# An encoder trunk on one core: turning a unit's products after the next block-sum step, and a third block-sum step in the sixteen-tile down pairs

## The chip, the cores and the metric

The kernel runs on one core of one Trainium2 chip. The metric is the device time of one execution in microseconds (us), the median of several runs. The core has five engines with queues of their own: TensorE (PE; PEld is its weight load), VectorE (DVE), ScalarE (ACT), GpSimd (POOL) and SyncE (SP). SP and POOL issue the transfers from the device's memory here.

## The reference

Two residual layers on a sequence of 256 tokens of width 2048, all in float32. Layer 0 mixes tokens by grouped-query attention, layer 1 by a gated linear recurrence. After each mixer comes the same gated feed-forward block, and only this block is touched by the change:

```python
D_MODEL, SEQ, DEPTH = 2048, 256, 2
D_FF = -(-8 * D_MODEL // (3 * 256)) * 256          # 5632

def swiglu(h, w_gate, w_up, w_down):
    return (jax.nn.silu(h @ w_gate) * (h @ w_up)) @ w_down

for i in range(DEPTH):
    h = rms_norm(x, norm_mix[i])
    x = x + (attention_mixer(h, ...) if i % 2 == 0 else recurrent_mixer(h, ...))
    x = x + swiglu(rms_norm(x, norm_ffn[i]), w_gate[i], w_up[i], w_down[i])
```

## The kernel before

**Three products for one.** A float32 number is split into a high part (rounded to the type that TensorE takes) and a low part (the rest). A product of two such numbers is three matmuls: high by high, high by low, low by high (`product` in `project_pair`). Each weight that comes from memory is therefore cast on ScalarE (`hi`) and subtracted on VectorE (`lo`), in `load_half`. A *half* is one load of 512 KB: two tiles of 128 rows by 512 columns. There are five buffers each for `raw`, `hi` and `lo`, so the preparation can run some halves ahead of TensorE.

**A pair.** `project_pair` computes two neighbouring outputs of 512 columns (j = 0 and 1) for all 256 tokens, in four accumulators. A *step* n takes the operand tiles 2n and 2n+1. A plain step has two halves, one for each j, with four products (12 matmuls) in each. `pair_plan` puts the first steps of a pair through both outputs together, and the rest first for j = 0, then for j = 1, so that output 0 can be finished early (`done(0, ...)`) while output 1 still runs.

**A block-sum step** replaces the eight products of a step by seven, from sums and differences of blocks, as Strassen's and Winograd's schemes do. Such a step needs sums of the weight blocks, which `seven_forms` prepares: one half comes through SP, the sum of two blocks through POOL, which loads one half and adds another to it during the transfer (tile `sr`, two buffers, fetched two block-sum steps ahead by `fetch_next`), and one quarter through SP again (`wx`). Three more blocks are made on VectorE (L307, L311, L312), and all are split into high and low parts (`wxh` and `wxl` are the three combined blocks, cast by L310 and L314, subtracted by L315 and L316; one buffer each). It also needs sums of the token blocks, made once for each step by `x_forms` (L325 to L330). Four of the seven products go to banks of their own, and after the last block-sum step of the pair `merge` (L382 to L386) combines them into `fg` and `fu`.

**The feed-forward block** (`ffn`) has 44 tiles of hidden features, in three groups (`PARTS`): 12, 16 and 16. A *unit* is a pair whose outputs are a gate and an up projection of four tiles, and so a group has 3, 4 or 4 units. All units but a layer's first have block-sum steps at n = 1, 3, 5, the first unit at 3 and 5. At its end, L842 adds the banks to the gate and a Silu follows on ScalarE, and L845 and L846 make the products `u` (tile `fu`). The products stand with tokens in the partitions, and the down projection wants features there. So they are *turned*: a transpose of 32 x 32 blocks on VectorE (L515), 16 copies of 32 x 256 between partitions on ScalarE (L523), then the split into a high and a low part (L857, L858). Then `x_forms` makes the token sums where the down pairs want them.

After a group's units come its two *down pairs* (`down`, c = 0 and 2), whose results are added to the residual stream `x_tok`. They have 6 steps in the first group (no block sums) and 8 in the others, with block-sum steps at n = 2 and 5. The second pair of layer 0's last group (`alone`) has none, since the next norm starts behind it.

**The order of the work.** TensorE's instructions run in the order in which the program writes them. Those of the other engines are ordered by a scheduler at build time, which takes from what is ready, the earlier written first, by its own timeline; each engine then runs its list in order. Two lines of order are given by hand: within the block, the weight casts on ScalarE follow each other, and the subtractions on VectorE too (`in_line`, `line`). `follow(i, j)` puts i behind j on the same engine.

Of the kernel before, what the change touches and what calls it, by code (L numbers as in the profile page):

```python
# [12 lines left out]
F32 = mybir.dt.float32  # L13
F32R = mybir.dt.float32r
AF = mybir.ActivationFunctionType
ALU = mybir.AluOpType
AX = mybir.AxisListType

P = 128
# [54 lines left out]
def trunk(ctx, tc, w, out):  # L74
# [79 lines left out]
    def down_plan(n, alone):  # L154
        if alone:
            return pair_plan(range(n), 0)
        return pair_plan(range(n), SHORT - 2 if n == SHORT else 1 + TWO[-1])
# [1 line left out]
    seven_at, ffn_ends = [], []  # L159

    def down_seven(n, alone):
        return () if alone or n == SHORT else TWO

    def ffn_order(l, base):
        units = [wide(f"w_gate{l}"), wide(f"w_up{l}")]
# [34 lines left out]
    def half():  # L200
        n = taken[0]
        taken[0] += 1
        if n == 0:
            load_x(0, 2)
            scale_x(0)
            return load_half(*order[n], 4, partial(load_x, 2, 2))
        if n == 1:
            scale_x(1)
            return load_half(*order[n], 2)
        if n < KT // 2:  # L210
            if n % 2 == 0:
                load_x(2 * n, 4)
            if n < KT // 2 - 1:
                scale_x(n)
        if n == KT // 2 - 2:
            scale_x(n + 1)
            load_tables()
        if n == KT // 2 + 2:
            tiles = load_half(*order[n])
            token_squares(1)  # L220
            return tiles
        return load_half(*order[n])
# [57 lines left out]
    def flat(t):  # L280
        return t.rearrange("p (k c) f -> p k (c f)", k=2)
# [39 lines left out]
    def x_forms(h0, h1, tag):  # L321
# [8 lines left out]
        dve.tensor_tensor(t[:, 1], y[:, 4:, :], t[:, 0].bitcast(F32), ALU.subtract)  # L330
        return [(t[:, 0, i, :], t[:, 1, i, :]) for i in range(4)]

    def project_pair(xs, forms, plan, middle, done):
        banks = [[], []]
        begun = set()

        def bank(j, a):
            while len(banks[j]) <= a:
                banks[j].append(new_acc())
            return banks[j][a]  # L340

        def product(acc, x, wt, last=False):
            for i, (a, b) in enumerate(((x[0], wt[0]), (x[0], wt[1]), (x[1], wt[0]))):
                pe.matmul(acc, a, b, start=id(acc) not in begun, stop=last and i == 2)  # L344
                begun.add(id(acc))
            step()
            step()

        def tokens(k, a):
            return [xs[k][:, o + a * P : o + (a + 1) * P] for o in (0, S)]  # L350

        seven = [n for n, cols in plan if n in forms]
        for n, cols in plan:
            if n in forms:
                s1, s2, s3, s4 = forms[n]
                b11, b21, t3, b22, t1, t2, t4 = seven_forms()
                if n == seven[0]:
                    p1, q6, q5, q7 = (ps_m.tile([P, WIDE], F32, tag="pm", name=nm("pm")) for _ in range(4))
                last = n == seven[-1]
                product(p1, tokens(2 * n, 0), b11, last)  # L360
                product(bank(0, 0), tokens(2 * n + 1, 0), b21)
                product(bank(1, 0), s4, b22)
                product(q7, s3, t3, last)
                product(q5, s1, t1, last)
                product(q6, s2, t2, last)
                product(bank(0, 1), tokens(2 * n + 1, 1), t4)
                if last:
                    middle(p1, q5, q6, q7)
                continue
            end = n == plan[-1][0]  # L370
            for j in cols:
                half()
                hi, lo = (flat(t) for t in newest["tiles"])
                for a in range(2):
                    for k in range(2):
                        product(bank(j, a), tokens(2 * n + k, a), (hi[:, k, :], lo[:, k, :]), end and k == 1)
                if end:
                    done(j, banks[j])
# [129 lines left out]

    def turned(src, both=True, behind=None, whole=False):
        b = fp[0].tile([P, 2, FOUR, P], F32, tag="tb", name=nm("tb"))
        f = fp[0].tile([P, 8, FOUR, 32], F32, tag="tf", name=nm("tf"))
        if whole:
            dve.transpose(b, src)  # L515
        for a in () if whole else range(2):
            dve.transpose(b[:, a, :, :], src[:, a, :])
        for q in range(4):
            for i in range(4):
                o, y = f[32 * i : 32 * i + 32, q::4, :, :], b[32 * q : 32 * q + 32, :, i, :]  # L520
                y = y.rearrange("p a (k t) -> p a k t", k=FOUR)
                turn = dve.tensor_copy if i % 2 and both else act.copy
                n = turn(o, y)  # L523
                if behind is not None:
                    follow(n, behind[i % 2])
        return f[:].rearrange("p q k t -> p k q t") if whole else [f[:, :, k, :] for k in range(FOUR)]

    fp = []

# [27 lines left out]
                norm.add(c)  # L557


    def down(xs, forms, norm=None, end=False):  # L560
        for c in (0, 2):
            def middle(*banks):
                g, u = merge(*banks)
                for j, t in enumerate((g, u)):
                    for a in range(2):
                        y = x_tok[:, a, c + j, :]
                        dve.tensor_tensor(y, y, t[:, a, :], ALU.add)

            def done(j, accs):
                for a in range(2):  # L570
                    n = 2 if end and c + j == NCOL - 1 else 1
                    for i in range(n):
                        sl = slice(i * WIDE // n, (i + 1) * WIDE // n)
                        y = x_tok[:, a, c + j, sl]
                        dve.tensor_tensor(y, y, accs[a][:, sl], ALU.add)
                        if end:
                            sync.dma_start(out=out[:, a, c + j, sl], in_=y)
                if norm is not None:
                    norm.add(c + j)

            alone = norm is not None and c > 0
            project_pair(xs, {} if alone else forms, down_plan(len(xs) // 2, alone), middle, done)


    prev = [None]
# [202 lines left out]
    def act_tiles():  # L788
        return xp.tile([P, FOUR, 2 * S], F32R, tag="act", name=nm("act"), bufs=4)
# [40 lines left out]
    def ffn(norm, nxt):  # L830
        coming[:] = [k for k in seven_at if taken[0] <= k < ffn_ends[taken[0] > ffn_ends[0]]]
        for _ in range(2):
            fetch_next()

        def unit(hid, forms, parts, i):
            got = []

            def done(j, accs):
                g, u = got
                for a, acc in enumerate(accs):  # L840
                    if j == 0:
                        dve.tensor_tensor(g[:, a, :], acc, g[:, a, :], ALU.add)  # L842
                        table_act(g[:, a, :], g[:, a, :], AF.Silu, scale=norm.rt[:, a : a + 1])
                    else:
                        dve.tensor_tensor(u[:, a, :], acc, u[:, a, :], ALU.add)  # L845
                        dve.scalar_tensor_tensor(u[:, a, :], u[:, a, :], norm.rt[:, a : a + 1], g[:, a, :], ALU.mult, ALU.mult)  # L846

            project_pair(norm.xs, {n: norm.forms[n] for n in unit_seven(i)}, unit_plan(i), lambda *banks: got.extend(merge(*banks)), done)
            if i == 0:
                n = THREE[0]  # L850
                norm.forms[n] = x_forms(norm.xs[2 * n], norm.xs[2 * n + 1], f"nf{n}")
            u = got[1]
            first = len(hid)
            f = turned(u, False, whole=True)
            h = act_tiles()
            hi, lo = (h[:, :, o : o + S].rearrange("p k (q t) -> p k q t", t=32) for o in (0, S))
            act.copy(hi, f)  # L857
            dve.tensor_tensor(lo, f, hi.bitcast(F32), ALU.subtract)  # L858
            hid.extend(h[:, k, :] for k in range(FOUR))
            for k, n in enumerate(TWO):  # L860
                if parts == KT and first <= 2 * n < len(hid):
                    forms[n] = x_forms(hid[2 * n], hid[2 * n + 1], f"hf{k}")

        line.update(act=None, dve=None)
        for p, n in enumerate(PARTS):
            hid, forms = [], {}
            for i in range(n // FOUR):
                unit(hid, forms, n, sum(PARTS[:p]) // FOUR + i)
            last = p == len(PARTS) - 1
            if last and nxt is not None:  # L870
                ln_exp_tables()
            down(hid, forms, nxt if last else None, last and nxt is None)
        line.clear()

    nr = Norm("norm_mix", KT)
# [218 lines left out]
```

## Time and profile before

| what | value |
|---|---|
| median of 3 runs | 1989.0 us (1987.55 to 1989.62) |
| the profiled execution's own time | 1986.64 us |
| its span in the trace | 1984.7 us |
| TensorE busy, matmuls | 1969.9 us, 9890 |
| VectorE busy | 1690.3 us (85% of the span) |
| ScalarE busy | 1346.5 us (68%) |
| GpSimd busy | 279.5 us (14%) |
| moved | 426.98 MB, 215 GB/s in the mean |
| granted TensorE clock | 1.0 |

The trace is of one execution; its times are counted from the span's start. A row of the timeline has the start, the duration, the engine, the line of the kernel, the operation with the tiles it writes and reads, how many instructions were put together, and in brackets how long the engine sat idle before it and what ended that. A row of the waits has the total, how often, and the longest. A row of the groups has the busy time, the mean of one in ns, and the idle time ahead. In the windows, the number in brackets is that of instructions. The matmuls overlap, so their spacing is read from their starts and not from their durations. The feed-forward blocks run from 267.6 to about 966 us and from 1284.3 us to the end.

### The profile page before, as it was taken

What the parts mean: (1) busy time and instruction counts of PE and PEld (TensorE: products, weight loads), DVE (VectorE), ACT (ScalarE), POOL (GpSimd) and SP (SyncE); (2) the same over time, 40 slices, a digit from 0 to 9 for tenths busy, and PEclk for the clock granted to TensorE, in tenths of its full rate; (3) what the DMA queues carried; (4) which work ended last, traced back from release to release, by engine and by line L of the source; (5) the groups of instructions that cost most, each with busy time, mean ns of one, the idle gap of its engine ahead of it and who ended that gap; (6) DMA issues with size and microseconds to landing.
All of it is one profiled execution on the core that took longest, in us unless ns stands there. A gap on an engine that the chain in (4) does not pass through costs nothing.

```text
span 1984.7 us, 28163 instructions
## 1 busy us (share of the span) xinstructions
PE 1969.9 (99%) x9890; PEld 1676.1 (84%) x9890; DVE 1690.3 (85%) x2355; ACT 1346.5 (68%) x2085; POOL 279.5 (14%) x369
## 2 busy tenths in 40 slices
PE   9999999999999999999999999999999999999999
PEld 8898888888887888888899998888888887888877
DVE  8998788857898888989878977898768998889986
ACT  7666666655777556777799987767646676567763
POOL 2563001000010010001034331001001010011000
PEclk9999999999999999999999999999999999999999
DMA  8444767767677777666655657566757777677773
GB/s 321 158 144 139 226 186 241 241 204 233 212 232 221 249 248 236 205 227 221 207 175 183 191 160 228 190 214 219 249 191 226 230 249 249 204 242 236 232 255 131
DMA packets 131469, 426.98 MB, mean 215 GB/s; under 512 B 14720, under 2 KB 15488, under 8 KB 131200
## 3 DMA queue, kind: packets, MB, share of 16 engines
q1 hardware_dynamic: 108720, 363.81, 53.5%
q0 software_dynamic: 22464, 61.35, 13.1%
q8 instruction: 78, 1.28, 0.3%
q14 instruction: 63, 0.52, 0.1%
q10 hardware_dynamic: 144, 0.02, 0.0%
HBM read 423.03 MB, written 2.10 MB: 214 GB/s over the span
## 4 chain that ended last, share of the span: by engine, by line
PE 72%; DVE 14%; issue 6%; ACT 5%; DMA 2%; POOL 0%; SPq 0%; DVEq 0%; ACTq 0%; POOLq 0%
PE acc L344 40%; PE acc L273 9%; PE pm L344 6%; DVE lo L133 5%; PE acc L251 4%; ACT tf L523 4%; PE acc L391 3%; PE acc L390 3%; PE acc L392 3%; DMA raw<-in_w_gate_dram 1%; PE pm L392 1%; PE pm L391 1%; PE pm L390 1%; DVE lo L313 1%; ACT wxh L314 1%
## 5 line engine op out<-in xcount | busy, mean ns | idle before, releaser
L133 DVE TENSOR_TENSOR lo<-raw,hi 128x1024 fp32r<-128x1024 f32 (+1 forms) x630 | 762.3, 1227 | 164.1 <-ACT hi L132 154.9
L132 ACT CAST hi<-raw 128x1024 fp32r<-128x1024 f32 (+1 forms) x630 | 647.8, 1044 | 346.4 <-PE acc L344 198.5
L344 PE MATMUL acc<-hi,xg 128*128 128x512 f32 x1920 | 613.7, 389 | 1.7 <-DVE fg L842 1.6
L344 PEld LDWEIGHTS acc<-hi,xg 128*128 128x128 f32 x1920 | 360.3, 188 | 77.9 <-DVE fg L842 2.5
L344 PE MATMUL acc<-hi,act 128*128 128x512 f32 x1212 | 378.8, 389 | 0.2 <-DVE fu L845 0.2
L344 PE MATMUL acc<-lo,xg 128*128 128x512 f32 x960 | 373.5, 389 | 0.0
L344 PEld LDWEIGHTS acc<-hi,act 128*128 128x128 f32 x1212 | 227.5, 188 | 47.9 <-issue 0.6
L344 PE MATMUL acc<-lo,act 128*128 128x512 f32 x606 | 235.8, 389 | 0.0
L344 PEld LDWEIGHTS acc<-lo,xg 128*128 128x128 f32 x960 | 180.2, 188 | 37.4
L523 ACT COPY tf<-tb 32x256 f32<-32x256 f32 x448 | 180.7, 403 | 30.7 <-DVE tb L515 24.8
L273 PE MATMUL acc<-hi,act 128*128 128x512 f32 x512 | 160.0, 390 | 0.0
L293 POOL DMA_DIRECT2D sr<-in_w_up_dram x64 | 35.5, 555 | 842.3 <-DVE lo L313 807.7
L391 PE MATMUL acc<-xg,hi 128*128 128x256 f32 x512 | 144.8, 283 | 0.6 <-DVE xg L468 0.6
L390 PE MATMUL acc<-xg,hi 128*128 128x256 f32 x512 | 144.9, 283 | 0.1
L392 PE MATMUL acc<-xg,lo 128*128 128x256 f32 x512 | 144.4, 282 | 0.0
L344 PEld LDWEIGHTS acc<-lo,act 128*128 128x128 f32 x606 | 113.7, 188 | 23.7
L251 PE MATMUL acc<-xg,hi 128*128 128x512 f32 x384 | 126.0, 397 | 0.1
L316 DVE TENSOR_TENSOR wxl<-raw,wxh 128x1024 fp32r<-128x1024 f32 x78 | 95.2, 1220 | 28.6 <-ACT wxh L314 28.6
L314 ACT CAST wxh<-raw 128x1024 fp32r<-128x1024 f32 x78 | 82.0, 1051 | 47.4 <-DVE raw L312 46.5
L273 PEld LDWEIGHTS acc<-hi,act 128*128 128x128 f32 x512 | 96.1, 188 | 19.6
L309 ACT CAST hi<-sr 128x1024 fp32r<-128x1024 f32 x78 | 82.0, 1051 | 44.6 <-PE acc L344 39.4
L273 PE MATMUL acc<-lo,act 128*128 128x512 f32 x256 | 99.6, 389 | 0.0
(246 smaller groups left out, 3289.2 us busy)
## 6 DMA issues: line engine op xcount, KB each, us to landing
raw<-in_w_gate_dram SPq DMA_DIRECT2D x176, 512.0 KB, 5.3
raw<-in_w_down_dram SPq DMA_DIRECT2D x162, 512.0 KB, 4.9
raw<-in_w_up_dram SPq DMA_DIRECT2D x112, 512.0 KB, 5.6
sr<-in_w_up_dram POOLq DMA_DIRECT2D x64, 512.0 KB, 4.7
raw<-in_w_in_dram SPq DMA_DIRECT2D x64, 512.0 KB, 4.4
raw<-in_w_qv_dram SPq DMA_DIRECT2D x40, 512.0 KB, 4.2
raw<-in_w_o_dram SPq DMA_DIRECT2D x32, 512.0 KB, 3.6
wx<-in_w_up_dram SPq DMA_DIRECT2D x64, 256.0 KB, 4.5
```

Of the source, the lines that this page charges most:

```text
L132: newest["cast"] = in_line("act", act.copy(hi[:, sl, :], raw[:, sl, :]))
L133: in_line("dve", dve.tensor_tensor(lo[:, sl, :], raw[:, sl, :], hi[:, sl, :].bitcast(F32), ALU.subtract))
L251: pe.matmul(o, w, x, start=(k == 0 and not part), stop=(k == total - 1 and not part))
L273: pe.matmul(accs[a], x, wt[:, k, :], start=(k0 + k == 0 and n == 0), stop=(end and k == 1 and n == 2))
L309: in_line("act", act.copy(hi, raw))
L314: in_line("act", act.copy(xh[:, 1:, :], r1))
L316: in_line("dve", dve.tensor_tensor(xl[:, 1:, :], r1, xh[:, 1:, :].bitcast(F32), ALU.subtract))
L344: pe.matmul(acc, a, b, start=id(acc) not in begun, stop=last and i == 2)
L390: pe.matmul(o, hi, x[:, :S], start=start, stop=False)
L391: pe.matmul(o, hi, x[:, S:], start=False, stop=False)
L392: pe.matmul(o, lo, x[:, :S], start=False, stop=stop)
L523: n = turn(o, y)
```

## The change

The turning is no longer written at a unit's end. Its six pieces (the transpose; four groups of four copies; the split with the token sums) are put into a list `owed`. The next `project_pair`, be it a unit's or a down pair's, takes them off: three after the preparation of each block-sum step, one after each half from the second step on, and all that are left ahead of the steps that go output by output. So in a pair with block-sum steps at n = 1 and 3, the transpose and eight copies stand behind the weights of step 1, four copies behind each half of step 2, and the split behind the weights of step 3. Each copy is put behind the last weight cast written by then.

In the sixteen-tile down pairs, the block-sum steps are n = 1, 3, 5 and no longer 2 and 5 (steps 2, 4 and 6, not 3 and 6, when counted from one). The order of the loads follows, and each group makes a third set of token sums.

```diff
     def down_seven(n, alone):
-        return () if alone or n == SHORT else TWO
+        return () if alone else () if n == SHORT else THREE
...
+    owed = []
+
+    def settle(n=1):
+        while owed and n:
+            owed.pop(0)()
+            n -= 1
+
     def project_pair(xs, forms, plan, middle, done):
...
-        for n, cols in plan:
+        for i, (n, cols) in enumerate(plan):
             if n in forms:
                 s1, s2, s3, s4 = forms[n]
                 b11, b21, t3, b22, t1, t2, t4 = seven_forms()
+                settle(3)
...
+            if len(cols) == 1:
+                settle(-1)
             end = n == plan[-1][0]
             for j in cols:
                 half()
+                if i:
+                    settle()
...
         def unit(hid, hid_units, forms, parts, i):
...
-            f = turned(u, False, whole=True)
-            h = act_tiles()
-            hi, lo = (h[:, :, o : o + S].rearrange("p k (q t) -> p k q t", t=32) for o in (0, S))
-            act.copy(hi, f)
-            dve.tensor_tensor(lo, f, hi.bitcast(F32), ALU.subtract)
-            hid.extend(h[:, k, :] for k in range(FOUR))
-            for k, n in enumerate(TWO):
-                if parts == KT and first <= 2 * n < len(hid):
-                    forms[n] = x_forms(hid[2 * n], hid[2 * n + 1], f"hf{k}")
+            first = FOUR * len(hid_units)
+            hid_units.append(i)
+            kept = {}
+
+            def transposes():
+                kept["b"], kept["f"] = (fp[0].tile([P, 2 * FOUR, P], F32, tag=n, name=nm(n), bufs=1) for n in ("tb", "tf"))
+                dve.transpose(kept["b"], got[1])
+
+            def copies(q):
+                b = kept["b"][:].rearrange("p (a i) (k t) -> p a i k t", a=2, k=FOUR)
+                f = kept["f"][:].rearrange("p q (k t) -> p q k t", k=FOUR)
+                for i in range(4):
+                    n = act.copy(f[32 * i : 32 * i + 32, q::4, :, :], b[32 * q : 32 * q + 32, :, i, :, :])
+                    follow(n, line["act"])
+
+            def split_tiles():
+                f = kept["f"][:].rearrange("p q (k t) -> p k q t", k=FOUR)
+                h = act_tiles()
+                hi, lo = (h[:, :, o : o + S].rearrange("p k (q t) -> p k q t", t=32) for o in (0, S))
+                act.copy(hi, f)
+                dve.tensor_tensor(lo, f, hi.bitcast(F32), ALU.subtract)
+                hid.extend(h[:, k, :] for k in range(FOUR))
+                for k, n in enumerate(THREE):
+                    if n in down_seven(parts // 2, False) and first <= 2 * n < len(hid):
+                        forms[n] = x_forms(hid[2 * n], hid[2 * n + 1], f"hf{k}")
+
+            owed.extend([transposes, *(partial(copies, q) for q in range(4)), split_tiles])
```

More of the change, by code (lines that the diff above doesn't have):

```diff
@@ L507, in spread, with turned @@
             return i
-    def turned(src, both=True, behind=None, whole=False):
+    def turned(src, both=True, behind=None):
         b = fp[0].tile([P, 2, FOUR, P], F32, tag="tb", name=nm("tb"))
         f = fp[0].tile([P, 8, FOUR, 32], F32, tag="tf", name=nm("tf"))
-        if whole:
-            dve.transpose(b, src)
-        for a in () if whole else range(2):
+        for a in range(2):
             dve.transpose(b[:, a, :, :], src[:, a, :])
@@ L525, in turned @@
                     follow(n, behind[i % 2])
-        return f[:].rearrange("p q k t -> p k q t") if whole else [f[:, :, k, :] for k in range(FOUR)]
+        return [f[:, :, k, :] for k in range(FOUR)]
     fp = []
@@ L557, in output, with down @@
                 norm.add(c)
-    def down(xs, forms, norm=None, end=False):
+    def down(n, xs, forms, norm=None, end=False):
         for c in (0, 2):
@@ L570, in done @@
                 for a in range(2):
-                    n = 2 if end and c + j == NCOL - 1 else 1
-                    for i in range(n):
-                        sl = slice(i * WIDE // n, (i + 1) * WIDE // n)
+                    m = 2 if end and c + j == NCOL - 1 else 1
+                    for i in range(m):
+                        sl = slice(i * WIDE // m, (i + 1) * WIDE // m)
                         y = x_tok[:, a, c + j, sl]
@@ L581, in down @@
             alone = norm is not None and c > 0
-            project_pair(xs, {} if alone else forms, down_plan(len(xs) // 2, alone), middle, done)
+            project_pair(xs, {} if alone else forms, down_plan(n // 2, alone), middle, done)
     prev = [None]
@@ L833, in ffn, with unit @@
             fetch_next()
-        def unit(hid, forms, parts, i):
+        def unit(hid, hid_units, forms, parts, i):
             got = []
@@ L851, in unit @@
                 norm.forms[n] = x_forms(norm.xs[2 * n], norm.xs[2 * n + 1], f"nf{n}")
-            u = got[1]
-            first = len(hid)
-            f = turned(u, False, whole=True)
-            h = act_tiles()
-            hi, lo = (h[:, :, o : o + S].rearrange("p k (q t) -> p k q t", t=32) for o in (0, S))
-            act.copy(hi, f)
-            dve.tensor_tensor(lo, f, hi.bitcast(F32), ALU.subtract)
-            hid.extend(h[:, k, :] for k in range(FOUR))
-            for k, n in enumerate(TWO):
-                if parts == KT and first <= 2 * n < len(hid):
-                    forms[n] = x_forms(hid[2 * n], hid[2 * n + 1], f"hf{k}")
+            first = FOUR * len(hid_units)
@@ L864, in ffn @@
+            owed.extend([transposes, *(partial(copies, q) for q in range(4)), split_tiles])
         line.update(act=None, dve=None)
         for p, n in enumerate(PARTS):
-            hid, forms = [], {}
+            hid, units, forms = [], [], {}
             for i in range(n // FOUR):
-                unit(hid, forms, n, sum(PARTS[:p]) // FOUR + i)
+                unit(hid, units, forms, n, sum(PARTS[:p]) // FOUR + i)
             last = p == len(PARTS) - 1
@@ L871, in ffn @@
                 ln_exp_tables()
-            down(hid, forms, nxt if last else None, last and nxt is None)
+            down(n, hid, forms, nxt if last else None, last and nxt is None)
         line.clear()
```

## The prediction, as it was made

> **What bounds the kernel now.** I read the page first, then the list of waits of TensorE, then the timelines of three engines around the places that list names, then the windows by stage. The page gives the frame:
>
> ```profile
> span 1984.7 us, 28163 instructions
> PE 1969.9 (99%) x9890; PEld 1676.1 (84%) x9890; DVE 1690.3 (85%) x2355; ACT 1346.5 (68%) x2085; POOL 279.5 (14%) x369
> ```
>
> PE is busy all the time, so the time is the number of matmuls times their spacing, plus the stalls. The spacing comes from the chain in order of time, in an undisturbed stretch:
>
> ```profile
> 267.62 21.76 PE acc L344 x96
> ```
>
> 21.76 / 96 = 0.2267 us for a matmul of 512 columns. A plain half is 12 of them (2.72 us), a plain step of two halves 24 (5.44), a block-sum step 7 x 3 = 21 (4.76). A unit with three such steps has 183 matmuls, 41.5 us; a sixteen-tile down pair now has two, 186 matmuls, 42.2 us. The stalls, from the waits of PE:
>
> ```profile
> PE pm L344 <- DVE wxl L316: 3.0, 4, 0.8
> PE pm L344 <- ACT wxh L314: 2.3, 4, 0.7
> PE acc L344 <- DVE fg L842: 1.6, 2, 0.9
> ```
>
> The first two are four places, one in each first down pair that follows a sixteen-tile group of units (there are four such groups). One of them on PE, then on ACT and DVE:
>
> ```profile
> 639.88 0.39 PE L344 MATMUL pm<-wxh,hf 128*128 128x512 f32 x1
> 640.81 0.50 PE L344 MATMUL pm<-wxh,hf 128*128 128x512 f32 x1 [0.54 <-ACT wxh L314]
> 642.07 0.50 PE L344 MATMUL pm<-wxl,hf 128*128 128x512 f32 x1 [0.76 <-DVE wxl L316]
> 642.41 0.40 PE L344 MATMUL pm<-wxh,hf 128*128 128x512 f32 x1
> ```
> ```profile
> 629.97 0.62 ACT L310 CAST wxh<-wx 128x512 fp32r<-128x512 f32 x1
> 633.06 6.63 ACT L523 COPY tf<-tb 32x256 f32<-32x256 f32 x16 [2.46 <-DVE tb L515]
> 639.71 1.05 ACT L314 CAST wxh<-raw 128x1024 fp32r<-128x1024 f32 x1
> ```
> ```profile
> 631.79 1.24 DVE L515 STREAM_TRANSPOSE tb<-fu 128x1024 f32<-128x1024 f32 x1
> 640.79 1.23 DVE L316 TENSOR_TENSOR wxl<-raw,wxh 128x1024 fp32r<-128x1024 f32 x1 [5.46 <-ACT wxh L314]
> ```
>
> The turning's sixteen copies (6.63 us) lie in ScalarE's queue between the two casts of the block-sum step's combined weights. PE starts at 640.81, 642.07 and 642.41 where the spacing would have given 640.11, then 0.2267 each: (0.93 + 1.26 + 0.34) - 3 x 0.23 = 1.84 us lost here, of which 1.30 is counted as idle. Four places: 7.4 us.
>
> **The change part by part.**
>
> *A third block-sum step.* Seven pairs take part (layer 0: two of the middle group, one of the last, as its other pair has none; layer 1: four). The loads confirm the count, two in each:
>
> ```profile
> sr<-in_w_down_dram POOLq DMA_DIRECT2D x14, 512.0 KB, 4.4
> sr<-in_w_down_dram POOLq DMA_DIRECT2D x14, 256.0 KB, 6.5
> ```
>
> They become 21 each. Seven steps x (24 - 21) x 0.2267 = 4.76 us of matmuls go; being PE's own work, they come off the end directly. By the Trainium skill's "TensorE: Matmul & The Clock Gate", section "Back-to-back issue gap", a sustained stream of 512-column matmuls runs at about 131 ns each, and 21 would be worth an estimated 2.75 us. This trace disagrees with 226.7 ns, and the measurement decides.
>
> *What the third step costs beside PE.*
>
> ```profile
> L133 DVE TENSOR_TENSOR lo<-raw,hi 128x1024 fp32r<-128x1024 f32 x624 | 759.6, 1234 | 163.7 <-ACT hi L132 154.7 <-DMA graw<-in_w_gates_dram 7.0
> L316 DVE TENSOR_TENSOR wxl<-raw,wxh 128x1024 fp32r<-128x1024 f32 x78 | 95.2, 1220 | 28.6 <-ACT wxh L314 28.6
> L311 DVE TENSOR_TENSOR raw<-sr,raw 128x512 f32<-128x512 f32 x78 | 53.8, 689 | 1.9
> L325 DVE TENSOR_TENSOR tb<-act 128x256 f32<-128x256 f32 x16 | 6.0, 416 | 0.0
> L327 DVE TENSOR_TENSOR tb<-tb 128x128 f32<-128x128 f32 x56 | 15.2, 283 | 0.1
> L330 DVE TENSOR_TENSOR hf<-tb,hf 128x512 fp32r<-128x512 f32 x8 | 5.4, 680 | 0.0
> ```
>
> On VectorE, four operations of 512 (0.69) and two of 1024 (1.22) are added and one subtraction of 1024 goes: 2.76 + 2.44 - 1.22 = 4.0 us for each step. Each group forms a third set of token sums: 2 x 0.42 + 4 x 0.28 + 0.68 = 2.6 us, in the group's second unit. On ScalarE a step adds one cast of 1024 and one of 512, 1.67 us by the 1.05 and 0.62 above, and a form one copy of 512. Whether this is hidden is read from the windows of one group: its third and fourth units, its first and second down pair.
>
> ```profile
> core 0: us, PE busy (x) PEld busy (x) DVE busy (x) ACT busy (x) POOL busy (x), PEclk, DMA share, GB/s
> 542.50:584.00 41.50, 41.50 (x184) 34.18 (x183) 38.12 (x49) 29.16 (x41) 4.23 (x6) 1.00 0.72 229
> 584.00:625.80 41.80, 41.80 (x184) 34.30 (x184) 39.56 (x52) 30.28 (x43) 4.25 (x6) 1.00 0.76 241
> 625.80:670.00 44.20, 42.91 (x188) 34.93 (x187) 38.19 (x45) 27.88 (x39) 2.82 (x4) 1.00 0.69 230
> 670.00:712.10 42.10, 42.10 (x188) 34.85 (x187) 34.07 (x40) 20.82 (x22) 2.83 (x4) 1.00 0.67 218
> ```
>
> ScalarE has room everywhere. VectorE has not: the first pair goes to 38.19 + 4.0 = 42.2 us of work in 41.5 us of matmuls, the second to 38.1. Neighbouring operations overlap by some 0.08 us, so the first figure is nearer 41.7. It is covered only by the lead that VectorE has over PE, and by the second pair's slack of 3.4 us. I expect a little of it to show.
>
> *The loads.* Per step SP issues 256 KB (wx) in place of 512, and POOL 512 and an accumulating 256 KB more: 0.5 MB a step, 3.7 MB in all. The down pairs then have the units' mix, which ran at 241 GB/s above without a wait of PE on a transfer. A unit also bounds the lateness of the POOL loads, whose buffer comes free two block-sum steps ahead:
>
> ```profile
> 587.61 1.21 DVE L313 TENSOR_TENSOR lo<-sr,hi 128x1024 fp32r<-128x1024 f32 x1
> 605.48 1.06 ACT L309 CAST hi<-sr 128x1024 fp32r<-128x1024 f32 x1
> ```
>
> From 588.8 to 605.5 are 16.7 us, and the two landings take 4.4 + 6.5 = 10.9: 5.8 us to spare. I cost the loads at nothing; without that cover each late microsecond is one of PE.
>
> *The turning moved behind the next block-sum step.* Its instructions are the same in number. Between units the transpose starts only when the products are there; the closest of those transitions:
>
> ```profile
> 592.28 1.23 DVE L515 STREAM_TRANSPOSE tb<-fu 128x1024 f32<-128x1024 f32 x1
> 601.81 1.22 DVE L316 TENSOR_TENSOR wxl<-raw,wxh 128x1024 fp32r<-128x1024 f32 x1 [0.26 <-ACT wxh L314]
> ```
> ```profile
> 588.67 2.94 ACT L132 CAST hi<-raw 128x1024 fp32r<-128x1024 f32 x3
> 593.54 6.63 ACT L523 COPY tf<-tb 32x256 f32<-32x256 f32 x16 [0.97 <-DVE tb L515]
> 600.20 0.62 ACT L310 CAST wxh<-wx 128x512 fp32r<-128x512 f32 x1
> ```
> ```profile
> 603.33 0.39 PE L344 MATMUL pm<-wxl,nf 128*128 128x512 f32 x1
> ```
>
> The next unit's first block-sum step and the casts of the step after it (588.67) are ahead of the copies already, so the new order demands nothing that isn't there: between units the move costs and gains about nothing. But look at the margin. The copies end at 600.2, the combined low parts of the second block-sum step at 603.03, and PE takes them at 603.33: 0.3 us. Into a down pair the move, with block-sum steps at 2, 4, 6, makes the same picture: the copies can no longer part the two casts of step 2, whose products begin 5.44 us into the pair, and must be done before those of step 4. So the four stalls go (-7.4), and what is late next is step 4's low part, with a margin like the 0.3 us above and a VectorE that carries 4.0 us more. I bound the new wait from nothing (the transition above) to 1.84 us a place (the wait of today), and take 0.7, nearer the first: 4 x 0.7 = 2.8. Into the short twelve-tile pair the tiles are wanted 8 halves in, 21.8 us; copies of 6.63 starting some 7 us in leave over 5 us. The two waits on fg (L842) are at the end of a layer's first unit, ahead of any deferred turning, and stay.
>
> **Sum.** -4.8 - 7.4 + 2.8 = -9.4 us. The profiled execution took 1986.64 us, so 1977.2 by its own time; the median of the three runs is 2.4 higher, 1989.0, and gives 1979.6. I take 1979.5.
>
> **Rivals.** *The stall only moves.* If the turn block parts or delays step 4's casts as it does step 3's today, or the engines' order comes out as before, the 7.4 stay in a new place and only the products go: 1989.0 - 4.8 = 1984.2. For it speaks the margin of 0.3 us, against it that none of the sixteen unit-to-unit transitions shows such a stall in the list of waits. Chance 0.22.
>
> *VectorE becomes the bound (slower).* In the fourth unit and the first pair it would have 39.6 + 41.7 us of work in 83 us of matmuls, and it sat idle for 5.46 us behind ScalarE's copies in that first pair. If that idle time stays and its lead is used up, PE waits for up to about 41.7 + 5.5 - 41.5 = 5.7 us in each of the four groups, 22.8 in all against the 12.2 gained: 1999.6. It decides from 12.2 / 4 = 3.05 us a group, and is over 0.2% slower from 4.05. Against it speaks the second unit's like load: the fourth unit had 39.56 us and PE did not wait. Chance 0.20, most of it short of the full price.
>
> *Late POOL loads (slower).* If each of the seven new steps waited 2 us for its sums, 14 us: 1979.5 + 14 = 1993.5. The Trainium skill's "SBUF — State Buffer", section "SBUF: two separate sides", has it that loads issued from GpSimd can be starved of descriptors while VectorE holds a port pair that both share. The landings of 4.4 and 6.5 us, with VectorE busy for 34 to 40 of 42 us, do not show it. Chance 0.03.
>
> **How the numbers follow.** The forecast has 0.55, with a range of its own from 1976.5 (no new wait) to 1983 (the full old wait in half the places). The range of 1975.5 to 1991 takes in the first rival and the second up to two microseconds over today, and the profiled run's lower base. About 0.2% (4 us) is what a measurement of this kernel can tell from no change. Faster by more: the forecast, 0.15 of the first rival and 0.01 of the second, 0.71. Within: 0.07 and 0.04 of these, 0.11. Slower: the second's remaining 0.15 and the third, 0.18.
>
> **What would show it.** Right: 21 matmuls fewer than 9890; loads of sr for down 21 twice; no wait of PE on wxh (L314's successor) at a first down pair's first block-sum step; VectorE near 41 us in that pair. Wrong: waits on wxl or on the accumulators' readers at the second block-sum step of units and pairs, more than 3 us a group; a wait of PE on sr; or copies that still lie between the two casts of wxh.

## The result and the profile after

The change took 1977.64 us (median, 1975.38 to 1979.94) against 1989.31 us (1987.55 to 1991.8) of the kernel before, run on the same chip: a ratio of 0.994 with a 95% interval of 0.9929 to 0.995. That is 11.7 us faster, where 9.4 was forecast (1979.5 us, range 1975.5 to 1991). The profiled executions differ by less, 1986.64 and 1978.20 us, or 8.4, since the one of before lies at the fast end of its runs.

The page of the changed kernel:

```profile
span 1976.4 us, 28257 instructions
PE 1964.0 (99%) x9869; PEld 1673.0 (85%) x9869; DVE 1721.8 (87%) x2418; ACT 1356.9 (69%) x2103; POOL 289.8 (15%) x383
```

There are 21 matmuls fewer, as counted, and 31.5 us more work on VectorE. TensorE's waits in the feed-forward blocks:

```profile
PE acc L351 <- DVE fg L852: 2.6, 2, 1.9
PE acc L351 <- DVE x_tok L585: 0.8, 1, 0.8
PE acc L351 <- DVE lo L133: 0.7, 1, 0.7
```

The waits on `wxh` and `wxl` are gone. What came up instead lies elsewhere than I had looked: on `fg` at the end of layer 1's first unit (1.9 of the 2.6 us, 0.9 before), and on `x_tok` and `lo` in layer 0's last two pairs. By the matmuls' starts against a spacing of 0.2267 us, the two feed-forward blocks lost 11.5 us before and 7.8 after. With the 4.8 us of matmuls saved this makes 8.5 us, against 8.3 by which the spans differ.

The start of the first sixteen-tile group's first down pair, where the first of the four stalls was, on ACT, on DVE and on PE:

```profile
625.35 0.62 ACT L310 CAST wxh<-wx 128x512 fp32r<-128x512 f32 x1 [1.26 <-DVE wx L307]
...
629.67 1.06 ACT L314 CAST wxh<-raw 128x1024 fp32r<-128x1024 f32 x1 [3.00 <-DVE raw L312]
...
634.43 6.62 ACT L875 COPY tf<-tb 32x256 f32<-32x256 f32 x16
641.08 0.62 ACT L310 CAST wxh<-wx 128x512 fp32r<-128x512 f32 x1
```
```profile
631.29 1.23 DVE L869 STREAM_TRANSPOSE tb<-fu 128x1024 f32<-128x1024 f32 x1
...
642.68 1.23 DVE L316 TENSOR_TENSOR wxl<-raw,wxh 128x1024 fp32r<-128x1024 f32 x1 [0.26 <-ACT wxh L314]
```
```profile
644.77 0.39 PE L351 MATMUL pm<-wxl,hf 128*128 128x512 f32 x1
```

Both casts of step 2's combined weights are done before the copies start, and the copies are done before those of step 4. The low part is there at 643.91 and used at 644.77: 0.86 us to spare, and no wait. The windows of the same group, from its fourth unit to its second down pair:

```profile
584.00:625.80 41.80, 41.80 (x186) 34.60 (x185) 39.46 (x50) 30.15 (x43) 4.25 (x6) 1.00 0.75 238
625.80:667.60 41.80, 41.80 (x186) 34.63 (x185) 39.76 (x48) 28.58 (x42) 4.24 (x6) 1.00 0.77 243
667.60:709.20 41.60, 41.60 (x186) 34.34 (x185) 39.23 (x47) 22.00 (x24) 4.25 (x6) 1.00 0.74 240
```

Behind the stretch and its length stand the busy times of PE, PEld and DVE, then ACT and POOL. The first pair now fits its 41.8 us, and VectorE is busy for 39 to 40 us in each of the three.

### The profile page after: what moved, and what is told of

Read it like the earlier page. It is cut to its first block, busy times and chain, and to the rows that moved or that the text cites. A ratio compares the mean times of both kernels' runs of the same rounds, so it can differ in the third digit from the quotient of the medians.

```text
span 1976.4 us, 28257 instructions
## 1 busy us (share of the span) xinstructions
PE 1964.0 (99%) x9869; PEld 1673.0 (85%) x9869; DVE 1721.8 (87%) x2418; ACT 1356.9 (69%) x2103; POOL 289.8 (15%) x383
## 4 chain that ended last, share of the span: by engine, by line
PE 92%; DVE 5%; issue 1%; ACT 1%; DMA 1%; POOL 0%; SPq 0%; DVEq 0%; ACTq 0%; POOLq 0%
PE acc L351 55%; PE pm L351 11%; PE acc L273 9%; PE acc L251 4%; PE acc L403 3%; PE acc L402 3%; PE acc L404 3%; DVE lo L133 2%; PE pm L404 1%; PE pm L403 1%; PE pm L402 1%; ACT hi L132 1%; DMA raw<-in_w_k_dram 0%; DMA raw<-in_w_gate_dram 0%; PE pm L778 0%
## 5 line engine op out<-in xcount | busy, mean ns | idle before, releaser
L133 DVE TENSOR_TENSOR lo<-raw,hi 128x1024 fp32r<-128x1024 f32 (+1 forms) x623 | 752.2, 1226 | 146.2 <-ACT hi L132 140.8
L132 ACT CAST hi<-raw 128x1024 fp32r<-128x1024 f32 (+1 forms) x623 | 638.6, 1044 | 296.2 <-PE acc L351 162.5
L351 PE MATMUL acc<-hi,act 128*128 128x512 f32 x1114 | 351.7, 389 | 1.1 <-DVE x_tok L585 0.8
L351 PEld LDWEIGHTS acc<-hi,act 128*128 128x128 f32 x1114 | 209.1, 188 | 45.9 <-DVE x_tok L585 1.7
L351 PE MATMUL acc<-lo,act 128*128 128x512 f32 x557 | 216.8, 389 | 0.7 <-DVE lo L133 0.7
L273 PE MATMUL acc<-hi,act 128*128 128x512 f32 x512 | 159.9, 390 | 0.0
L875 ACT COPY tf<-tb 32x256 f32<-32x256 f32 x352 | 142.2, 404 | 15.2 <-DVE tb L869 11.3
L351 PEld LDWEIGHTS acc<-lo,act 128*128 128x128 f32 x557 | 104.6, 188 | 22.7 <-DVE lo L133 1.2
L309 ACT CAST hi<-sr 128x1024 fp32r<-128x1024 f32 x85 | 89.4, 1052 | 41.3 <-PE acc L351 29.3
L310 ACT CAST wxh<-wx 128x512 fp32r<-128x512 f32 x85 | 52.7, 620 | 88.8 <-DVE wx L307 57.9
L273 PEld LDWEIGHTS acc<-hi,act 128*128 128x128 f32 x512 | 96.1, 188 | 19.7
L316 DVE TENSOR_TENSOR wxl<-raw,wxh 128x1024 fp32r<-128x1024 f32 x85 | 103.6, 1219 | 7.9 <-ACT wxh L314 7.7
```

Source lines behind the costliest of these rows:

```text
L132: newest["cast"] = in_line("act", act.copy(hi[:, sl, :], raw[:, sl, :]))
L133: in_line("dve", dve.tensor_tensor(lo[:, sl, :], raw[:, sl, :], hi[:, sl, :].bitcast(F32), ALU.subtract))
L273: pe.matmul(accs[a], x, wt[:, k, :], start=(k0 + k == 0 and n == 0), stop=(end and k == 1 and n == 2))
L309: in_line("act", act.copy(hi, raw))
L316: in_line("dve", dve.tensor_tensor(xl[:, 1:, :], r1, xh[:, 1:, :].bitcast(F32), ALU.subtract))
L875: n = act.copy(f[32 * i : 32 * i + 32, q::4, :, :], b[32 * q : 32 * q + 32, :, i, :, :])
```

## The experiments

### Each half of the change by itself

Two things were changed at once, and a third, the place of the first block-sum step, came with one of them. My theory gave the lost stalls to both together; another theory gives them to the place alone.

**The turning behind, and nothing else**, in the changed kernel:

```diff
-        return () if alone else () if n == SHORT else THREE
+        return () if alone else () if n == SHORT else TWO
...
-                for k, n in enumerate(THREE):
+                for k, n in enumerate(TWO):
```

> Only the turning is put behind the next block-sum step; the down pairs keep block-sum steps 3 and 6. Theory 1 (the turning's copies in front of the second cast of the combined weights make the four stalls, and moving them behind takes the stalls away): the four waits on wxh and wxl (5.3 us idle, 7.4 us by the starts) go or shrink to under 2 us, 1982 to 1984 us. Theory 2 (the place of the block-sum step decides, the move of the turning by itself brings nothing): the four waits stay, on those or on neighbouring tiles, 1987 to 1991 us.

Measured: 1988.59 us, ratio 0.9996 (0.9988 to 1.0005), no change. The waits of PE, and ScalarE's queue at the place of the first stall:

```profile
PE acc L351 <- DVE lo L133: 3.0, 4, 0.8
PE acc L351 <- ACT hi L132: 1.7, 4, 1.0
```
```profile
633.27 1.66 ACT L875 COPY tf<-tb 32x256 f32<-32x256 f32 x4 [2.46 <-DVE tb L869]
634.96 1.05 ACT L314 CAST wxh<-raw 128x1024 fp32r<-128x1024 f32 x1
636.04 4.97 ACT L875 COPY tf<-tb 32x256 f32<-32x256 f32 x12
641.03 3.90 ACT L132 CAST hi<-raw 128x1024 fp32r<-128x1024 f32 x4
```

The order by hand did what it says: only four copies stand ahead of the second cast, and the wait on it is gone. But the other twelve now stand ahead of the next plain halves, which are as late as the combined weights were. The four stalls moved on to the next plain halves and nearly kept their size (6.9 us by the starts, 7.4 before). This is my first rival, in a kernel I had not thought of for it.

**The third block-sum step, and nothing else**, in the kernel before:

```diff
-        return () if alone or n == SHORT else TWO
+        return () if alone or n == SHORT else THREE
...
-            for k, n in enumerate(TWO):
+            for k, n in enumerate(THREE):
```

> Only block-sum steps 2, 4 and 6 in the sixteen-tile down pairs; the turning stays written at the unit's end. Theory 1: the copies still part the casts of some block-sum step; the products' 4.8 us go and the stalls stay, about 1984 us, with four waits on wxh and wxl in the first down pairs. Theory 2: with the first block-sum step one earlier its casts are ready ahead of the turning anyway, as between units; products and stalls both go, 1976 to 1979 us, the same as the whole change.

Measured: 1976.93 us, ratio 0.9936 (0.9924 to 0.9948), as the whole change. Its list of waits has none on `wxh` or `wxl`. Theory 2 holds.

**Block-sum steps 2 and 6 in place of 3 and 6**, as many matmuls as before:

```diff
-THREE, TWO, SHORT = (1, 3, 5), (2, 5), 6
+THREE, TWO, SHORT = (1, 3, 5), (1, 5), 6
```

> The kernel before with block-sum steps 2 and 6 in place of 3 and 6 in the sixteen-tile down pairs: as many matmuls as before, turning as before. Theory 1: no gain, 1987 to 1991 us. Theory 2: the four stalls go without any saved product, 1989.3 - 7.4 = about 1982 us.

Measured: 1978.56 us, ratio 0.9943 (0.993 to 0.9955). Moving one step by one place, without saving a product, gives nearly all of the change's gain. It is 3.4 us faster than theory 2 asked for; the spans of the two profiles (1984.7 and 1976.7 us) differ by 8.0, which the four stalls nearly fill. Its ScalarE queue at the same place shows why they are gone:

```profile
630.13 1.05 ACT L314 CAST wxh<-raw 128x1024 fp32r<-128x1024 f32 x1 [2.34 <-DVE raw L312]
631.09 3.90 ACT L132 CAST hi<-raw 128x1024 fp32r<-128x1024 f32 x4
635.96 6.63 ACT L523 COPY tf<-tb 32x256 f32<-32x256 f32 x16 [0.97 <-DVE tb L515]
```

The copies cannot start before the unit's products are there and transposed: they start 7.2 us into the pair in the kernel before, and 9.7 here. A step that begins 5.4 us into the pair has its casts behind it by then, and four plain halves follow before the copies come. A step that begins 10.9 us in has its weights caught by them. The only waits of some size left in the two blocks are the 1.6 us on `fg`, as before, and the starts lose 2.8 us in all.

So the third step's own gain is the difference between these two kernels: 1.6 us by the medians, 1.2 by the spans (1976.7 and 1975.5), though it takes away 4.8 us of matmuls. The intervals of the two ratios overlap, so its size is uncertain. By the starts, the two blocks lose 2.8 us without it and 6.9 with it: 4.1 us are given back as new waits, and 0.7 us of gain are left within the blocks.

### Where the third step's gain goes

**The change again**, unaltered, for a second profile.

> The changed kernel once more, for a second profile. If the waits of its first profile at the end of layer 1's first unit (3.8 us by the starts) and in layer 0's last down pairs (2.1 us) belong to its order of instructions, they come again within a few tenths; if they came from a late transfer in that one execution, they shrink to what the kernel before has there (1.1 and 0). Time 1975 to 1980 us.

Measured: 1977.39 us. The new waits came again: on `x_tok` 0.7 and on `lo` 1.0 in layer 0's last pairs, on `fg` at the end of layer 1's first unit 1.6, and one on `fu` ahead of layer 1's short pair (0.7). The first three belong to the change; the last is not in its first profile, so that isn't shown of it. At the end of layer 1's first unit the starts lose some 1.8 us now and not 3.8, since the first profile also had 1.6 us of slow matmuls there (last section).

**Six pairs**: the first down pair of layer 0's last group keeps two block-sum steps, 2 and 6; the order of the loads and the token sums follow it.

```diff
-    def down_seven(n, alone):
-        return () if alone else () if n == SHORT else THREE
+    def down_seven(n, alone, near=False):
+        return () if alone or n == SHORT else (1, 5) if near else THREE
...
```

> The change, but the first down pair of layer 0's last group has block-sum steps 2 and 6 only, 3 matmuls more than the change. If the two waits in layer 0's last two pairs (2.1 to 2.3 us by the starts) come from VectorE, which the third step leaves late when the next norm's work starts, they go: 1977.4 + 0.7 - 2.2 = about 1976 us. If they come from the norm's work alone, they stay: 1978 us.

Measured: 1976.31 us, ratio 0.9932 (0.9919 to 0.9944). Its waits:

```profile
PE acc L352 <- DVE fg L853: 1.4, 2, 0.7
PE acc L352 <- DVE fu L856: 1.0, 3, 0.5
PE acc L352 <- DVE x_tok L586: 0.8, 1, 0.8
```

The two waits in layer 0's last pairs are gone, and the kernel with the third step and the old turning has both, so the third step makes them. Both were on VectorE, which has the next norm's work beside it there. In time this kernel isn't separated from the change, since the intervals of the ratios overlap. The wait on `x_tok` in this list is another, between the two pairs of layer 0's middle group. **Once more for a second profile**:

> The six-pair kernel once more. The same question: 0.70 us idle at the end of layer 1's first unit in its first profile, and a wait of 0.79 us on x_tok between the two pairs of layer 0's middle group. If they belong to the kernel, both come again within 0.15 us; if they vary by execution, not.

One time of 1974.40 us. The wait on `fg` was 0.70 again; that on `x_tok` 0.41, so this one varies by execution.

**The longer wait on `fg` in layer 1's first unit.** No third step is near it, and SP issues the loads there at the same moments in every kernel so far, to 0.3 us. They land later. ScalarE waits for one of them, in the change:

```profile
1316.11 1.05 ACT L132 CAST hi<-raw 128x1024 fp32r<-128x1024 f32 x1 [1.41 <-DMA raw<-in_w_gate_dram]
```

In that stretch, 28 to 38 us behind the block's first matmul, the gate weights' loads took 5.3 us (median of four) in the kernel before, 5.4 with steps 2 and 6, and 6.5 in the change. One thing that differs everywhere is where the tiles lie, since the third token sums need 4 KB in each partition. **An idle tile** tests that, in the kernel with steps 2 and 6:

```diff
+        if tag == "hf1":
+            pool.memset(fp[1].tile([P, 2, 4, P], F32, tag="idle", name=nm("idle"), bufs=1)[:, 0, 0, 0:1], 0.0)
         t = fp[1].tile([P, 2, 4, P], F32R, tag=tag, name=nm(tag), bufs=1)
```

> Block-sum steps 2 and 6 with the old turning (as many matmuls as before), and an idle tile of 4 KB in each partition where the third token sums would lie, touched once a group by a one-column write of GpSimd. Theory A (the longer wait at the end of layer 1's first unit, 1.8 to 2.2 us by the starts against 1.0 to 1.1, and the late loads ahead of it come from where the tiles lie): the wait grows to 1.7 us or more, and the time by 1 us to about 1979.5. Theory B (they come from the third step's work itself or what follows from it): the wait stays at 1.0 to 1.1, and the time at 1978.5 as without the tile.

Measured: 1978.60 us, as theory B has it, and a wait of 1.39 us (1.6 by the starts): between both forecasts, with loads of 5.8 us. **The same kernel without the tile, again**:

> Block-sum steps 2 and 6 with the old turning, once more, for the wait at the end of layer 1's first unit (0.87 us idle in its first profile). If that wait belongs to a kernel, 0.8 to 0.95 us again, as in the kernel before and in the kernel with the turning behind only; if it varies from execution to execution by itself, anything from 0.7 to 1.9.

One time of 1978.69 us, and 1.11 us where its first profile had 0.87. So the wait varies by 0.24 us between executions of this kernel, and by 0.36 between those of the change (1.92 and 1.56); 0.3 to 0.5 more for the tile says little. Over the kernels it was 0.86 to 1.11 without a third step and without the tile (four profiles), 1.56 to 1.94 with the step in seven pairs (four, with the kernel of the next section), and 0.70 with it in six (two). The traces tell which load it is: the gate half issued 29.6 us behind the block's first matmul. In the six profiles where the wait is over 1 us, this half lands 35.2 to 36.0 us behind that matmul, and the wait is its landing less 34.08 us, to 0.01 us. Why it lands later is left open.

### How much room the turning has

**Two more transposes** of the same products at each of the 22 unit ends, in the changed kernel:

```diff
-                dve.transpose(kept["b"], got[1])
+                for _ in range(3):
+                    dve.transpose(kept["b"], got[1])
```

> The change with two more transposes of the same products ahead of the copies at each of the 22 unit ends, 2 x 1.16 us of VectorE each; they write what the first wrote. If the chain of transpose, copies and the second block-sum step's weights is what comes next, with its margin of about 0.9 us in the profile of the change, TensorE waits 2.3 - 0.9 = 1.4 us at the twelve transitions with token sums and some 0.5 us at the other eight: 1977.4 + 21 = about 1998 us, waits on wxl and wxh of 15 us or more. If VectorE's lead covers it, no wait is over 0.5 us and the time stays under 1981.

Measured: 2076.30 us, ratio 1.0435 (1.042 to 1.0449), 99 us more than the change and not 21. The direction was right and the size wrong by nearly five. PE's waits, then DVE and ACT at the first down pair already shown:

```profile
PE pm L351 <- ACT wxh L314: 46.1, 20, 3.2
PE pm L351 <- DVE wxl L316: 15.0, 20, 0.8
```
```profile
652.88 1.24 DVE L870 STREAM_TRANSPOSE tb<-fu 128x1024 f32<-128x1024 f32 x1
...
660.28 1.24 DVE L870 STREAM_TRANSPOSE tb<-fu 128x1024 f32<-128x1024 f32 x1
```
```profile
660.47 0.62 ACT L310 CAST wxh<-wx 128x512 fp32r<-128x512 f32 x1 [4.37 <-DVE wx L307]
661.55 6.63 ACT L876 COPY tf<-tb 32x256 f32<-32x256 f32 x16 [0.45 <-DVE tb L870]
668.20 1.04 ACT L314 CAST wxh<-raw 128x1024 fp32r<-128x1024 f32 x1
```

The three transposes were not issued in a row. The build put other work of VectorE between them, the last came 7.4 us behind the first, and the copies fell between the two casts again, now those of the following block-sum step. All 20 turnings with such a step behind them pay 3.1 us of idle time in the mean (61.1 in all). By the starts, the two blocks lose 101.7 us where the change lost 7.8: some 79 at the waits, and 21 in matmuls at a lower clock (last section). So in this one test the room was about one instruction's place in a queue, not an amount of time that is used up evenly.

### A version that needs less

**Six pairs, and each layer's first unit with its last block-sum step one place earlier**, so that two halves lie between the first output's end and the next unit:

```diff
-FIRST_STEPS = (0, 1, 2, 4, 3, 6, 5, 7)
+FIRST_STEPS = (0, 1, 2, 4, 3, 5, 6, 7)
```

> The six-pair kernel, and each layer's first unit with its last block-sum step one earlier (steps in the order 0, 1, 2, 4, 3, 5, 6, 7 and no longer 0, 1, 2, 4, 3, 6, 5, 7), so that two halves and not one lie between the first output's end and the next unit. The waits on fg there (L852; 1.0 us in layer 0 and 1.8 to 2.2 in layer 1 by the starts) should go, 1976 - 3 = 1973 us. Against it: step 5 then needs its token sums 5.4 us earlier, just behind the norm; if they come late, TensorE waits there instead and the time is 1976 or more.

Measured: 1975.18 us, ratio 0.9921 (0.9909 to 0.9934). The forecast was 1973. In layer 1 the wait on `fg` is gone; in layer 0 it stayed (0.8 us), and one of 0.2 us on `wxl` came up in each layer's second unit. **The same without the deferral**, the turning written at the unit's end as in the kernel before:

> The kernel with six pairs and the first unit's order 0, 1, 2, 4, 3, 5, 6, 7, but with the turning written at the unit's end as in the kernel before. If the deferral is worth nothing wherever the first block-sum step is the second step, the same time as with it, 1974 to 1976.5 us. If it is worth something once other waits are gone, 1977 us or more.

Measured: 1974.92 us (1973.02 to 1975.46), ratio 0.9923 (0.9909 to 0.9937), the same time as with the deferral. This is the fastest profile of all (span 1971.2 us), and it has none of the deferral's code. It beats the kernel before. Against the change its median is 2.5 to 2.7 us better, but the intervals of the two ratios overlap, so that is not shown.

## Why the prediction was right, and where it was not

- **The products.** 21 matmuls and 4.76 us were right as work. I let all of it reach the end, apart from 2.8 us of new waits in the first down pairs. Measured, 1.2 us arrive by the spans and 1.6 by the medians, with overlapping intervals: the step gives back 4.1, and none of that at the second block-sum step of a first pair, where I looked for it.
- **The four stalls, -7.4 us.** They went, as forecast, and the page's line of waits named the right tiles. The reason was half wrong. I wrote that "the copies can no longer part the two casts of step 2" as the work of the move and of the steps' new place together. The deferral alone leaves four copies between them, too few for a wait, and gains nothing, since the other twelve hold up the halves behind. The place alone does it all. The transitions between units, which I had quoted as the closest likeness, pointed to that already: their first block-sum step is the second step, the old turning was in front of them, and none stalled on `wxh` or `wxl`.
- **The deferral between units, about nothing.** Right, and it holds for the whole change: with and without it, 1977.39 and 1976.93 us on one chip.
- **The next margin.** I took 0.3 us from the closest transition and expected 0.7 us of wait at each of four places; the first place has 0.86 us to spare, and no place waits.
- **VectorE.** 41.7 us were forecast for the first pair and 38.1 for the second; 39.8 and 39.2 were measured. The sum for the group was near (39.5 + 39.8 + 39.2, with its fourth unit ahead), so some of the first pair's work seems to be done a pair later. This rival did not decide, though the two waits of layer 0's last pairs, on VectorE, are of its kind on a small scale.
- **Late POOL loads.** No wait of TensorE on `sr` shows. In layer 1's first unit the accumulating load took 8.0 us against 6.7 before, but it was the gate's load by SP that ScalarE waited for there.
- **The total.** -4.8 - 7.4 + 2.8 came out near in part by luck: the 2.8 us of new waits, put in the wrong place, stood for 4.1 us in others. About 3 us of the medians' difference are in no profile: the kernel before ran from 1986.6 to 1993.7 us in its 17 runs beside the first experiments, and the one with steps 2 and 6 from 1977.5 to 1978.9 in five. Whether the stalls themselves vary so much can't be told from one profile of before.
- **The forecast's own range.** Its upper end was reckoned wrongly: the full old wait in half of the four places is 2 x 1.84 = 3.7 us in place of 2.8, which gives 1980.4 us and not 1983.

## What to carry to other kernels

When a change does two things, look for a place in the trace of before where one of them is already there: here every unit but a layer's first began like the new down pair, and none stalled on the combined weights. A block of work that becomes ready at a fixed time stalls whichever weights are due just behind it, so it is cheaper to have the costly step ahead of that time than to sort the block's pieces in the queue. And with another engine nine tenths busy, most of the work saved on the bounding engine came back here as waits; measure what is left of it by itself.

## What the runs showed of the hardware

TensorE's clock falls after waits much shorter than I had thought of. The kernel with two more transposes, after waits of 2.29 and 0.61 us with one matmul between them (the last three numbers are the granted clock, the DMA share and GB/s):

```profile
668.00:670.00 2.00, 0.65 (x1) 0.19 (x1) 0.72 (x1) 1.98 (x3) 0.78 (x1) 0.87 0.15 57
...
672.00:674.00 2.00, 2.00 (x6) 1.61 (x5) 2.00 (x3) 1.98 (x3) 0.00 (x0) 0.50 1.08 346
...
676.00:678.00 2.00, 2.00 (x10) 1.60 (x9) 1.97 (x3) 0.99 (x2) 0.00 (x0) 0.92 0.31 127
```

From 669.49 to 676.31 us the granted clock is 0.50, and the matmuls follow each other at 0.43 us. In the change's first profile, one wait of 1.92 us stands ahead of such a stretch:

```profile
1323.00:1325.50 2.50, 0.69 (x4) 0.23 (x2) 2.50 (x5) 2.14 (x3) 0.55 (x1) 1.00 0.00 0
1325.50:1330.00 4.50, 4.39 (x12) 3.48 (x13) 4.50 (x7) 1.77 (x2) 0.32 (x1) 0.62 0.79 226
```

There the slow matmuls cost 1.6 us on top of the 2.1 lost by the wait. It isn't the length of the wait alone that decides. With the third step alone, a wait of 1.94 us at the same place left the clock at 1.00. And the kernel with two more transposes has almost the same two waits, 1.42 or 1.43 us and then 0.76, once in each layer's second unit; the clock stayed at 1.00 behind them in layer 0 and fell in layer 1:

```profile
331.60:337.60 6.00, 5.20 (x22) 4.08 (x23) 5.98 (x6) 5.36 (x6) 0.20 (x1) 1.00 0.84 206
1395.10:1401.10 6.00, 5.16 (x14) 3.92 (x15) 5.93 (x6) 5.36 (x7) 0.15 (x1) 0.72 0.83 209
```

What decides is not shown, but the traces show a beat. In the change's first profile the clock is first full at 5.20 us, halves at 1326.15 (387 x 3.413 us later) and is full again at 1329.57 (3.41 later). In the kernel with two more transposes, too, every change of the clock lies a whole multiple of 3.413 us behind the one before. So where in such a stretch a wait falls may matter; no run varied that by itself. The Trainium skill's "TensorE: Matmul & The Clock Gate", section "HAM oscillation — how this bites in real kernels", puts the edge at gaps above about 3.4 us; no single wait in these two blocks was longer than 3.19 us, and the measurement decides.
